# Routing of a two-layer mixture-of-experts block: the chain on PSUM, one comparison per one-hot matrix, the tokens' low parts behind it

## Chip, cores and metric

One core of one Trainium2 chip. The metric is the device time of one execution in microseconds (us), the median over several runs; lower is better. The five engines are named as the profile names them: PE (matrix), DVE (vector), ACT (scalar), POOL (GpSimd) and SP (whose queue issues nearly all DMAs); SPq is SP's queue, PEld the load of a matmul's stationary operand.

## What is computed

Two layers over 256 tokens x and 256 context tokens, width 1024. Each layer mixes tokens (gating, bidirectional retention) and then sends every token to 2 of 32 experts. The first layer routes 512 tokens, the second only the 256 of x. Cut to the routing:

```python
g_top, g_sel = lax.top_k(hf @ w_group + b_group, 1)            # 4 groups
e_in_group = take_along_axis(e_logits, g_sel)                  # 8 experts of that group
e_top, e_sel = lax.top_k(e_in_group, 2)
weights = p_group * softmax(e_top)
expert_id = g_sel * 8 + e_sel
y = sum over the 2 choices of weight * (silu(h @ w1[e]) * (h @ w3[e])) @ w2[e]
```

## The kernel before, in words

Tokens stand in tiles of 128: `nt` is 4 in layer 0 and 2 in layer 1. `split` (nt == 4) says that the tokens `h2[t]` are cut into a high part `h2h[t]` (ACT, `first_part`) and a low part `h2l[t]` (`second_part`, one subtraction of 128x1024), and that dispatch multiplies both with the one-hot matrices; in layer 1 `h2[t]` is used whole.

**Before the routing.** The last quarter of the output projection is made token tile by token tile. An order written out as a string sets what PE does: `o0` to `o3` are the four tiles (24 matmuls each, `out_tile`), `t` turns a finished tile for the router (`turned`, two transposes and an ACT copy) and finishes its norm (`final`, with a power on POOL, L186), `l` multiplies it with the router's weights into the PSUM bank `lob` (`logits`, L955), `r` and `R` do the same for the third quarter. After each tile DVE runs `residual` (L933, L935, L937).

**The routing chain on DVE**, L1046 to L1078: logits are summed and scaled in the SBUF tile `lr`, biases are added into `lo`; the best group by MAX8 and FIND_INDEX8 (`gm`, `gi`), its index as a float (`gf`, L1061), a mask over the groups (`goh`, L1063 and L1065), the masked logits (L1067), the two best experts (`em`, `ei`, `ef`), their one-hot rows `oh`, and the sum `ohs` in bf16. All of these tiles lie in SBUF. PE then counts with a triangular matrix how many earlier tokens chose each expert (`pp`, L1084) and the totals (`pc_`, L1088). At the same time POOL adds the shift to the last tile (`scaled`, L1003) and makes the low parts of tiles 0 to 2 (L1011, 128x1024 each); the low part of tile 3 is made on DVE behind the one-hot matrices.

**Places.** An expert has CAP = 64 places. DVE picks each choice's place out of `pp` (L1107, L1109), turns it into a slot number (`slot`, L1114, L1115), and `place` (L1119, L1120) builds the one-hot matrix `pm` of 128 slots with two comparisons per token tile against `iota`. In layer 0 four experts (a quad, 256 slots) are dispatched together (`quad_places`, `quad_block`, L1184), in layer 1 two (`pair_places`, `dispatch_some`, L1129). ACT copies the dispatched tokens into `xg`; then `expert` runs (`w1`, `w3`: L1220; `w2`: L1237), `weighted` scales (L1246, L1247), `collect` returns the result to the tokens (L1255, L1261, and additions on POOL, L1262).

**Order of work.** PE and SP run in program order. From the start of the routing to `routing.close()` DVE, ACT and POOL do too; after it a scheduler orders them. SP issues the experts' weights (0.5 MB each, 12 an expert) in one queue into a ring of buffers (`pump`); each waits until its buffer is free, and the next wait behind it. Some of these buffers held `h2[t]` before.

Of the kernel before, what the change touches and what calls it, by code (L numbers as in the profile page):

```python
# [21 lines left out]
P = 128  # L22
# [29 lines left out]
def hybrid_kernel(  # L52
# [481 lines left out]
    for l in range(depth):  # L534
# [451 lines left out]
        def out_tile(t):  # L986
            o = bank()
            for k in range(KD):
                ah, al = (a[:, t % 2 * P:(t % 2 + 1) * P] for a in mT[t // 2][k])
# [57 lines left out]
        V.tensor_tensor(out=lrv, in0=lrv, in1=rs4[:, 0:nt, None].to_broadcast([P, nt, 36]), op=ALU.mult)  # L1047
        V.tensor_tensor(out=lo[:, 0:nt, 0:36].rearrange("p (s t) e -> p s t e", t=2), in0=lrv.rearrange("p (s t) e -> p s t e", t=2),
# [12 lines left out]
        V.tensor_copy(gf[:, 0:nt], gi[:, 0:nt, 0:1])  # L1061
        goh = small([P, 4, GROUPS], tag="goh", bufs=1)
        V.tensor_tensor(out=goh[:, 0:nt], in0=iota[:, None, 0:GROUPS].to_broadcast([P, nt, GROUPS]),  # L1063
                        in1=gf[:, 0:nt].to_broadcast([P, nt, GROUPS]), op=ALU.is_equal)
        V.tensor_scalar(out=goh[:, 0:nt], in0=goh[:, 0:nt], scalar1=-LOW, scalar2=LOW, op0=ALU.mult, op1=ALU.add)  # L1065
# [3 lines left out]
                        in1=goh[:, 0:nt, :, None].to_broadcast([P, nt, GROUPS, PER_GROUP]), op=ALU.add)  # L1069
# [4 lines left out]
        V.tensor_copy(ef[:, 0:nt], ei[:, 0:nt, 0:2])  # L1074
        V.tensor_tensor(out=oh[:, 0:nt].rearrange("p t j e -> p (t j) e"),
                        in0=iota[:, None, 0:EXPERTS].to_broadcast([P, 2 * nt, EXPERTS]),
                        in1=ef[:, 0:nt].rearrange("p t j -> p (t j)")[:, :, None].to_broadcast([P, 2 * nt, EXPERTS]), op=ALU.is_equal)
        V.tensor_tensor(out=ohs[:, 0:nt], in0=oh[:, 0:nt, 0], in1=oh[:, 0:nt, 1], op=ALU.add)  # L1078
# [10 lines left out]

        negm = small([P, 4, 1], tag="negm", bufs=1)  # L1090
# [14 lines left out]
        pos = small([P, 8], tag="pos", bufs=1)
        for j in range(2):
            V.tensor_tensor(out=sel[:, 0:nt, j], in0=oh[:, 0:nt, j], in1=pp[:, 0:nt * EXPERTS].rearrange("p (t e) -> p t e", e=EXPERTS),  # L1107
                            op=ALU.mult)
        V.tensor_reduce(out=pos[:, 0:W], in_=selv, axis=X, op=ALU.add)  # L1109
        isov = small([P, 8], tag="isov", bufs=1)  # L1110
        V.tensor_scalar(out=isov[:, 0:W], in0=pos[:, 0:W], scalar1=float(CAP), scalar2=None, op0=ALU.is_ge)

        slot = small([P, 8], tag="slot", bufs=1)
        V.scalar_tensor_tensor(out=slot[:, 0:W], in0=efv, scalar=float(CAP), in1=pos[:, 0:W], op0=ALU.mult, op1=ALU.add)  # L1114
        V.scalar_tensor_tensor(out=slot[:, 0:W], in0=isov[:, 0:W], scalar=65536.0, in1=slot[:, 0:W], op0=ALU.mult, op1=ALU.add)  # L1115

# [49 lines left out]
        def quad_places(q):  # L1166
            pm = a4t((P, 4, 256), F32R)
            for i in range(2):
                base = small([P, 8], tag="base")
                V.tensor_scalar(out=base[:, 0:W], in0=slot[:, 0:W], scalar1=-128.0 * (2 * q + i), scalar2=None, op0=ALU.add)  # L1170
                place(base, P, pm[:, :, i * P:(i + 1) * P])
# [397 lines left out]
```

## Time and profile before

| | |
|---|---|
| median of 3 runs | 1930.32 us (1927.92 to 1930.35) |
| the profiled execution's own time | 1926.31 us |
| its span | 1924.5 us |
| busy in the span | PE 94%, DVE 50%, ACT 33%, POOL 27% |
| granted TensorE clock, mean | 0.977 |
| routing of layer 0, of layer 1 | about 563 to 594 us, about 1425 to 1443 us |

The span is what the trace covers; the device time of the same execution is 1.8 us longer. A timeline row gives start, duration, engine, line, operation, output<-input, count, and in brackets how long the engine stood idle before it and what ended that.

### The profile page before, as it was taken

The numbers are of one execution on the slowest core, as the hardware profiler recorded it, in microseconds if no ns is written. First come the engines' busy times: TensorE is split into PE (matmuls) and PEld (weight loads), VectorE is DVE, ScalarE is ACT, GpSimd is POOL, SyncE is SP. The second block draws the span as 40 slices with busy tenths as digits, with TensorE's granted clock in tenths as the row PEclk, the third lists the DMA queues.
The fourth block names the chain that finished last, engine by engine and source line by source line (L and its number), as shares of the span: only waits on it lengthen the run. The fifth ranks groups of instructions, "written<-read, shape, count | busy, mean of one in ns | idle before, by whom it ended". The sixth has DMA issues, their size and how long they took to land. (4 is left out here: it accounts for less than half of the span.)

```text
span 1924.5 us, 28311 instructions
## 1 busy us (share of the span) xinstructions
PE 1810.2 (94%) x10899; PEld 1238.4 (64%) x10899; DVE 958.7 (50%) x1748; ACT 629.6 (33%) x1012; POOL 524.3 (27%) x417
## 2 busy tenths in 40 slices
PE   7999998899977999999999889999979999999996
PEld 5988898798974444444444389999964444444442
DVE  4878575564554334333433377885562232232223
ACT  3645454443332121222122254444432221222222
POOL 1444353432030233232424242132021122122121
PEclk9999999899998999999999899999989999999998
DMA  9445343344765999999999549863798999999995
GB/s 342 133 165 181 121 154 126 115 154 148 207 227 179 396 405 402 402 402 403 406 402 391 188 162 321 281 197 122 233 346 306 406 409 409 409 409 408 409 409 220
DMA packets 234111, 553.49 MB, mean 288 GB/s; under 512 B 23121, under 2 KB 118513, under 8 KB 233970
## 3 DMA queue, kind: packets, MB, share of 16 engines
q1 hardware_dynamic: 233586, 551.57, 77.1%
q8 instruction: 88, 1.44, 0.3%
q14 instruction: 53, 0.43, 0.1%
q0 software_dynamic: 384, 0.05, 0.0%
HBM read 550.45 MB, written 1.10 MB: 287 GB/s over the span
## 5 line engine op out<-in xcount | busy, mean ns | idle before, releaser
L1262 POOL TENSOR_TENSOR u<-u,t 128x512 f32<-128x512 f32 x184 | 229.4, 1281 | 749.3 <-DVE t L1261 749.0
L1220 PE MATMUL mm<-u,a 128*64 128x512 f32 x1376 | 333.6, 593 | 1.4 <-ACT a L1132 1.4
L207 DVE TENSOR_TENSOR wlo<-raw,whi 128x1024 fp32r<-128x1024 f32 x157 | 218.2, 1392 | 152.1 <-ACT whi L206 151.7
L247 PE MATMUL mm<-u,wlo 128*128 128x256 f32 (+1 forms) x800 | 268.7, 336 | 5.4 <-DVE wlo L207 5.4
L245 PE MATMUL mm<-u,whi 128*128 128x256 f32 (+1 forms) x800 | 269.9, 337 | 0.0
L246 PE MATMUL mm<-u,whi 128*128 128x256 f32 (+1 forms) x800 | 267.6, 334 | 0.0
L1247 DVE SCALAR_TENSOR_TENSOR a<-mm,sw,a 64x512 fp32r<-64x512 f32 x128 | 95.9, 749 | 335.8 <-ACT a L1246 335.5
L245 PE MATMUL mm<-whi,u 128*128 128x256 f32 x832 | 240.0, 288 | 1.9 <-ACT u L569 1.5
L247 PE MATMUL mm<-whi,u 128*128 128x256 f32 x832 | 237.9, 286 | 0.8 <-DVE u L571 0.4
L246 PE MATMUL mm<-wlo,u 128*128 128x256 f32 x832 | 237.1, 285 | 0.8 <-DVE wlo L207 0.8
L1220 PEld LDWEIGHTS mm<-u,a 128*64 128x64 f32 x1376 | 106.3, 137 | 195.8 <-issue 178.1
L206 ACT ACTIVATE whi<-raw 128x1024 fp32r<-128x1024 f32 x160 | 169.7, 1063 | 170.3 <-PE mm L246 62.5
L1261 DVE TENSOR_TENSOR t<-mm,u 128x512 f32<-128x512 f32 x190 | 119.6, 675 | 135.2 <-PE mm L1255 134.8
L247 PEld LDWEIGHTS mm<-u,wlo 128*128 128x128 f32 x800 | 151.9, 190 | 22.7 <-DVE wlo L207 7.5
L245 PEld LDWEIGHTS mm<-whi,u 128*128 128x128 f32 x832 | 161.0, 193 | 6.8 <-issue 3.3
L1246 ACT ACTIVATE a<-mm,sw 64x512 fp32r<-64x512 f32 x128 | 87.3, 682 | 235.4 <-PE mm L1237 187.3
L245 PEld LDWEIGHTS mm<-u,whi 128*128 128x128 f32 x800 | 152.0, 190 | 17.2 <-issue 1.6
L1237 PE MATMUL mm<-u,t 128*64 128x512 f32 x664 | 157.3, 610 | 5.9 <-ACT t L1231 5.9
L247 PEld LDWEIGHTS mm<-whi,u 128*128 128x128 f32 x832 | 160.8, 193 | 2.2 <-DVE u L571 1.0
L246 PEld LDWEIGHTS mm<-wlo,u 128*128 128x128 f32 x832 | 161.0, 194 | 1.3 <-DVE wlo L207 1.2
L246 PEld LDWEIGHTS mm<-u,whi 128*128 128x128 f32 x800 | 152.0, 190 | 14.4
L1223 ACT ACTIVATE t<-mm 64x512 f32<-64x512 f32 x64 | 38.0, 594 | 322.3 <-PE mm L1220 322.3
(309 smaller groups left out, 2625.3 us busy)
## 6 DMA issues: line engine op xcount, KB each, us to landing
u<-in_w_dram SPq DMA_DIRECT2D x510, 512.0 KB
raw<-in_w_in_dram SPq DMA_DIRECT2D x96, 512.0 KB
raw<-in_w_dram SPq DMA_DIRECT2D x75, 512.0 KB
whi<-in_w_dram SPq DMA_DIRECT2D x73, 512.0 KB
wlo<-in_w_dram SPq DMA_DIRECT2D x73, 512.0 KB
a<-in_w_ada_dram SPq DMA_DIRECT2D x57, 512.0 KB
u<-in_w_ada_dram SPq DMA_DIRECT2D x39, 512.0 KB
a<-in_w_dram SPq DMA_DIRECT2D x37, 512.0 KB
```

The costliest lines, as they stand in the source:

```text
L206: S.activation(hi, rv, AF.Copy)
L207: low_by[0].tensor_tensor(out=lo, in0=rv, in1=hi.bitcast(F32), op=ALU.subtract)
L245: T.matmul(out, lhsT=sh, rhs=mh, start=first, stop=False)
L246: T.matmul(out, lhsT=sh, rhs=ml, start=False, stop=False)
L247: return T.matmul(out, lhsT=sl, rhs=mh, start=False, stop=last)
L1220: T.matmul(o[h * 64:(h + 1) * 64, :], lhsT=x[:, s0:s0 + 64], rhs=w(k), start=(k == 0), stop=(k == KD - 1), tile_position=(0, 64 * h))
L1223: S.activation(hh[0:64], o[64:128, :], AF.Silu)
L1237: T.matmul(o[n % banks][n * 64:(n + 1) * 64, :], lhsT=hTt[:, s], rhs=wc(s)[:, n * 512:(n + 1) * 512], start=(s == 0), stop=(s == 3), tile_ ...
L1246: S.activation(dh, src, AF.Copy, scale=w)
L1247: V.scalar_tensor_tensor(out=dl, in0=src, scalar=w, in1=dh.bitcast(F32), op0=ALU.mult, op1=ALU.subtract)
L1261: V.tensor_tensor(out=y, in0=o, in1=g2[t // 2][:, hs], op=ALU.mult)
L1262: eng.tensor_tensor(out=res[t][:, hs], in0=res[t][:, hs], in1=y, op=ALU.add)
```

## The change

1. In layer 0 the order string becomes `o0 r o1 R t0 o2 l0 t1 s0 O3 l2 t3 s1 l3`: tile 3 (`O3`) takes the logits of tile 1 and the turning of tile 2 between its matmuls. `scaled_at_once` (DVE) serves tiles 0 and 1; tiles 2 and 3 go by `scaled` (ACT, then POOL).
2. The chain's intermediate values lie in the bank `lob`.
3. `pp` plus one, times `ohs`, gives each token's place per expert (`far`, in `lob`; `where`, a copy in SBUF for later). `slots` builds a one-hot matrix with one comparison of this with 1 to 64.
4. POOL makes the low part of tile 0 only; tiles 1 to 3 are made on DVE behind the first one-hot matrices, and PE takes all high parts before the low ones.
5. What only the overflow needs (`pos`, `isov` and on) moves to `blocks()`; `routing.close()` comes after it.

```diff
-        for op in ("o0 r o1 R t0 o2 l0 t1 o3 l1 t2 l2 t3 l3" if nt == 4 else "o0 r t0 o1 R l0 t1 l1").split():
+        for op in ("o0 r o1 R t0 o2 l0 t1 s0 O3 l2 t3 s1 l3" if nt == 4 else "o0 r t0 o1 R l0 t1 l1").split():
...
+            elif op[0] == "O":
+                gate_c = out_tile(t, {2: lambda: last_logits(1), 5: lambda: last_turned(2)})
...
-        scaled(nt - 1)
+        for t in range(nt - 2, nt):
+            scaled(t)
         pump(PRE[l][2])
         if split:
             for t in range(nt):
                 first_part(t)
-            for t in range(nt - 1):
-                second_part(t, G)
-        lrv = lr[:, 0:nt]
-        V.tensor_tensor(out=lrv, in0=lrv, in1=lob[:, 0:nt * 36].rearrange("p (t e) -> p t e", e=36), op=ALU.add)
...
+            second_part(0, G)
+
+        lrv, lobv = lr[:, 0:nt], lob[:, 0:nt * 36].rearrange("p (t e) -> p t e", e=36)
+        V.tensor_tensor(out=lobv, in0=lobv, in1=lrv, op=ALU.add)
...
-        gf = small([P, 4, 1], tag="gf", bufs=1)
+        gf = lob[:, 144:144 + nt].rearrange("p (t o) -> p t o", o=1)
...
-        goh = small([P, 4, GROUPS], tag="goh", bufs=1)
+        goh = lob[:, 160:160 + nt * GROUPS].rearrange("p (t g) -> p t g", g=GROUPS)
...
+        far = lob[:, 0:nt * EXPERTS].rearrange("p (t e) -> p t e", e=EXPERTS)
+        V.scalar_tensor_tensor(out=far, in0=pp[:, 0:nt * EXPERTS].rearrange("p (t e) -> p t e", e=EXPERTS), scalar=1.0, in1=ohs[:, 0:nt],
+                               op0=ALU.add, op1=ALU.mult)
+        where = lr[:, :, 0:EXPERTS]
+
+        def slots(e0, n, pm, src, ts):
+
+            V.tensor_tensor(out=pm[:, ts, 0:n * CAP].rearrange("p t (e s) -> p t e s", e=n),
+                            in0=iota[:, None, None, 1:CAP + 1].to_broadcast([P, ts.stop - ts.start, n, CAP]),
+                            in1=src[:, ts, e0:e0 + n, None].to_broadcast([P, ts.stop - ts.start, n, CAP]), op=ALU.is_equal)
+
+        if split:
+            pm = a4t((P, 4, 256), F32R)
+            slots(0, 4, pm, far, slice(0, 2))
+            slots(0, 4, pm, far, slice(2, 4))
+            for t in range(1, nt):
+                second_part(t, V)
+        else:
+            pm = t2t((P, 4, P), F32R)
+            slots(0, 2, pm, far, slice(0, nt))
...
+            held0 = [bank() for _ in range(2)]
+            for part in range(2):
+                for k in range(4):
+                    for t in range(nt):
+                        T.matmul(held0[k // 2][:, k % 2 * 256:(k % 2 + 1) * 256],
...
-                routing.close()
...
                     blocks()
                     if last:
                         row_everywhere(g2[0])
+                    routing.close()
```

The instructions at three places. First DVE in layer 0, from the logits to the masked logits; `mm_5122` is the bank `lob`, `rs` the four norm factors, `rc` the biases. Before:

```order
L1046 TENSOR_TENSOR lr_4655<-lr_4655,mm_5122 128x144
L1047 TENSOR_TENSOR lr_4655<-lr_4655,rs_761_5121 128x144
L1048 TENSOR_TENSOR lo_601<-lr_4655,rc 128x4x36
L1057 MAX gm_5343<-lo_601 128x8 x4
L1059 MAX_INDEX gi_5344<-gm_5343,lo_601 128x8 x4
L1061 CAST gf_5355<-gi_5344 128x4
L1063 TENSOR_TENSOR goh_5357<-iota,gf_5355 128x16
L1065 TENSOR_SCALAR goh_5357<-goh_5357 128x16
L1067 TENSOR_TENSOR lr_4655<-lo_601,goh_5357 128x4x32
```

and now:

```order
L1056 TENSOR_TENSOR mm_5122<-mm_5122,lr_4655 128x144
L1057 TENSOR_TENSOR mm_5122<-mm_5122,rs_761_5121 128x144
L1058 TENSOR_TENSOR lo_601<-mm_5122,rc 128x4x36
L1067 MAX gm_5340<-lo_601 128x8 x4
L1069 MAX_INDEX gi_5341<-gm_5340,lo_601 128x8 x4
L1071 CAST mm_5122<-gi_5341 128x4
L1073 TENSOR_TENSOR mm_5122<-iota,mm_5122 128x16
L1075 TENSOR_SCALAR mm_5122<-mm_5122 128x16
L1077 TENSOR_TENSOR lr_4655<-lo_601,mm_5122 128x4x32
```

The same nine steps in the same order; seven of them now read or write the bank, and none of these seven reads two tiles of SBUF.

Second, DVE in layer 0 behind the counts of PE (`mm_5368` is `pp`, `a_800` the first `pm`, `u_801` to `u_803` the low parts of tiles 1 to 3), as it is now:

```order
L1104 SCALAR_TENSOR_TENSOR mm_5122<-mm_5368,ohs_4657 128x128
L1110 TENSOR_TENSOR a_800_5385<-iota,mm_5122 128x512 x2
L1013 TENSOR_TENSOR u_801_5388<-u_698_4651,u_790_5329 128x1024
L1013 TENSOR_TENSOR u_802_5390<-u_699_4652,u_791_5331 128x1024
L1013 TENSOR_TENSOR u_803_5392<-u_700_4653,u_792_5333 128x1024
L1125 COPY lr_4655<-mm_5122 128x4x32
L1127 TENSOR_SCALAR negm_5395<-gm_5340 128x4
L1131 TENSOR_TENSOR dex_5399<-em_5342 128x4
```

Three instructions stand where some thirty stood (with the sixteen comparisons L1119 and L1120 among them); behind them come three low parts instead of one, and `negm`, on which the exponentials of ACT (L1097, now L1133) wait, has moved from before the counts to behind the low parts.

Third, PE in layer 0 at the first dispatch. `u_789` to `u_792` are the high parts, `u_793` and on the low ones. Before (the first eight of 32):

```order
L1184 MATMUL mm_5434<-a_812_5409,u_789_5326 128x256
L1184 MATMUL mm_5434<-a_812_5409,u_793_5334 128x256
L1184 MATMUL mm_5434<-a_812_5409,u_790_5328 128x256
L1184 MATMUL mm_5434<-a_812_5409,u_794_5336 128x256
L1184 MATMUL mm_5434<-a_812_5409,u_791_5330 128x256
L1184 MATMUL mm_5434<-a_812_5409,u_795_5338 128x256
L1184 MATMUL mm_5434<-a_812_5409,u_792_5332 128x256
L1184 MATMUL mm_5434<-a_812_5409,u_817_5432 128x256
```

and now the last four of the sixteen high ones and the first four low ones:

```order
L1295 MATMUL mm_5411<-a_800_5385,u_789_5327 128x256
L1295 MATMUL mm_5411<-a_800_5385,u_790_5329 128x256
L1295 MATMUL mm_5411<-a_800_5385,u_791_5331 128x256
L1295 MATMUL mm_5411<-a_800_5385,u_792_5333 128x256
L1295 MATMUL mm_5410<-a_800_5385,u_793_5335 128x256
L1295 MATMUL mm_5410<-a_800_5385,u_801_5388 128x256
L1295 MATMUL mm_5410<-a_800_5385,u_802_5390 128x256
L1295 MATMUL mm_5410<-a_800_5385,u_803_5392 128x256
```

The eighth matmul needed the last low part; now the twentieth does.

## Rows read from the trace of the kernel before

**Rows 1.** Timeline, PE, layer 0: start us, us, work [idle before, releaser].

```profile
565.45 0.64 PE L955 MATMUL mm<-wr,t 128*128 128x36 f32 x4 [1.23 <-ACT t L949]
...
580.53 0.21 PE L1084 MATMUL mm<-ohs,upper 128*128 128x32 bf16 x1 [13.09 <-DVE ohs L1078]
...
586.06 2.31 PE L1184 MATMUL mm<-a,u 128*128 128x256 f32 x7 [4.98 <-DVE a L1120]
588.86 4.78 PE L1184 MATMUL mm<-a,u 128*128 128x256 f32 x25 [0.49 <-DVE u L1011]
593.57 1.94 PE L1220 MATMUL mm<-u,a 128*64 128x512 f32 x8
...
607.71 0.43 PE L1229 MATMUL mm<-ident,t 64*128 64x64 f32 x4 [1.58 <-DVE t L1224]
```

**Rows 2.** Timeline, DVE, layer 0.

```profile
563.64 0.43 DVE L933 TENSOR_TENSOR mm<-mm,t 128x256 f32<-128x256 f32 x1 [0.67 <-PE mm L247]
...
568.82 2.35 DVE L1048 TENSOR_TENSOR lo<-lr,rc 128x144 f32<-128x144 f32 x1
...
572.16 1.25 DVE L1061 CAST gf<-gi 128x4 f32<-128x4 uint32 x1
573.44 2.27 DVE L1063 TENSOR_TENSOR goh<-iota,gf 128x16 f32<-128x16 f32 x1
575.74 2.26 DVE L1065 TENSOR_SCALAR goh<-goh 128x16 f32<-128x16 f32 x1
578.04 0.29 DVE L1067 TENSOR_TENSOR lr<-lo,goh 128x128 f32<-128x128 f32 x1
...
580.18 0.29 DVE L1078 TENSOR_TENSOR ohs<-oh 128x128 bf16<-128x128 f32 x1
...
587.59 1.22 DVE L1011 TENSOR_TENSOR u<-u,u 128x1024 fp32r<-128x1024 f32 x1
...
606.17 0.69 DVE L1209 TENSOR_REDUCE sw<-mm 64x1 f32<-64x2 f32 x4 [4.14 <-PE mm L1205]
```

**Rows 3.** Timeline, POOL, layer 0, the routing.

```profile
568.62 2.39 POOL L1003 TENSOR_TENSOR u<-u,u 128x1024 f32<-128x1024 f32 x1 [1.26 <-ACT u L1002]
570.97 7.00 POOL L1011 TENSOR_TENSOR u<-u,u 128x1024 fp32r<-128x1024 f32 x3
```

**Rows 4.** Timeline, DVE, layer 0, in the experts.

```profile
670.12 4.25 DVE L1261 TENSOR_TENSOR t<-mm,u 128x512 f32<-128x512 f32 x7
```

**Rows 5.** Timeline, POOL, layer 0, in the experts.

```profile
669.68 9.93 POOL L1262 TENSOR_TENSOR u<-u,t 128x512 f32<-128x512 f32 x8 [22.96 <-DVE t L1261]
```

**Rows 6.** Timeline, ACT, layer 0: the first and the last of the exponentials.

```profile
580.59 0.30 ACT L1097 ACTIVATE ge<-lo,negm 128x4 f32<-128x4 f32 x1 [6.96 <-DVE negm L1091]
...
582.15 0.19 ACT L1098 ACTIVATE dex<-dex 128x4 f32<-128x4 f32 x1
```

**Rows 7.** Timeline, DVE, layer 1, the routing.

```profile
1429.20 2.26 DVE L1048 TENSOR_TENSOR lo<-lr,rc 128x72 f32<-128x72 f32 x1
...
1432.11 1.58 DVE L1061 CAST gf<-gi 128x2 f32<-128x2 uint32 x1
```

**Rows 8.** Timeline, PE, layer 1, the routing.

```profile
1435.89 0.19 PE L1084 MATMUL mm<-ohs,upper 128*128 128x32 bf16 x1 [7.32 <-DVE ohs L1078]
...
1438.38 3.91 PE L1129 MATMUL mm<-t,u 128*128 128x128 f32 x16 [2.20 <-DVE t L1120]
```

**Rows 9.** Timeline, POOL, layer 1, the routing.

```profile
1428.99 4.67 POOL L1003 TENSOR_TENSOR u<-u,u 128x1024 f32<-128x1024 f32 x2 [0.87 <-ACT u L1002]
```

**Rows 10.** Stretches: busy us of each engine, granted clock, DMA share, GB/s.

```profile
591.00:593.00 2.00, 2.00 (x13) 2.00 (x13) 0.00 (x0) 0.60 (x1) 0.00 (x0) 0.67 0.33 133
...
1750.00:1800.00 50.00, 49.32 (x256) 21.90 (x254) 14.04 (x33) 10.94 (x19) 5.28 (x5) 1.00 1.03 408
```

**Rows 11.** Waits of SP's queue, 560:1060: us in total, times, longest.

```profile
SPq L274 <- PE mm L1237: 168.9, 112, 5.6
```

**Rows 12.** The same in layer 1, 1400:1924.

```profile
SPq L274 <- DMA u<-in_w_dram: 188.3, 210, 1.9
```

More of the change, by code (lines that the diff above doesn't have):

```diff
@@ L984, in hybrid_kernel, with out_tile @@
         pump(PRE[l][1])
-        def out_tile(t):
+        def out_tile(t, amid=None):
             o = bank()
             for k in range(KD):
+                if amid and k in amid:
+                    amid[k]()
                 ah, al = (a[:, t % 2 * P:(t % 2 + 1) * P] for a in mT[t // 2][k])
@@ L1073, in hybrid_kernel @@
             V.max_index(ei[:, t], em[:, t], ein[:, t])
[L1074 to L1078, printed above, removed]
+        W = 2 * nt
+        efp = lob[:, 192:192 + W].rearrange("p (t j) -> p t j", j=2)
+        V.tensor_copy(efp, ei[:, 0:nt, 0:2])
+        ohp = lob[:, 320:320 + nt * EXPERTS].rearrange("p (t e) -> p t e", e=EXPERTS)
+        for j, dst in ((1, ohp), (0, oh[:, 0:nt, 0])):
+            V.tensor_tensor(out=dst, in0=iota[:, None, 0:EXPERTS].to_broadcast([P, nt, EXPERTS]),
+                            in1=efp[:, :, j:j + 1].to_broadcast([P, nt, EXPERTS]), op=ALU.is_equal)
+        V.tensor_tensor(out=ohs[:, 0:nt], in0=ohp, in1=oh[:, 0:nt, 0], op=ALU.add)
         pp = bank()
@@ L1088, in hybrid_kernel @@
             T.matmul(pc_[:, 0:EXPERTS], lhsT=ones_bf, rhs=ohs[:, t], start=(t == 0), stop=(t == nt - 1))
+        far = lob[:, 0:nt * EXPERTS].rearrange("p (t e) -> p t e", e=EXPERTS)
[15 more added lines that the diff above has]
+            slots(0, 2, pm, far, slice(0, nt))
+        V.tensor_copy(where[:, 0:nt], far)
         negm = small([P, 4, 1], tag="negm", bufs=1)
@@ L1098, in hybrid_kernel @@
         S.activation(dex[:, 0:nt], dex[:, 0:nt], AF.Exp)
-        W = 2 * nt
-        sel = t2t((P, 4, 2, EXPERTS))
-        selv = sel[:, 0:nt].rearrange("p t j e -> p (t j) e")
+        V.tensor_copy(oh[:, 0:nt, 1], ohp)
+        V.tensor_copy(ef[:, 0:nt], efp)
         ohv = oh[:, 0:nt].rearrange("p t j e -> p (t j) e")
         efv = ef.rearrange("p t j -> p (t j)")[:, 0:W]
[L1105 to L1115, printed above, removed]
         def place(base, n, dst):
@@ L1167, in quad_places @@
             pm = a4t((P, 4, 256), F32R)
[L1168 to L1171, printed above, removed]
+            slots(4 * q, 4, pm, where, slice(0, nt))
             return pm
@@ L1190, in pair_places @@
         def pair_places(pr):
-            base = small([P, 8], tag="base")
-            V.tensor_scalar(out=base[:, 0:W], in0=slot[:, 0:W], scalar1=-128.0 * pr, scalar2=None, op0=ALU.add)
-            return places(base, P)
+            pm = t2t((P, 4, P), F32R)
+            slots(2 * pr, 2, pm, where, slice(0, nt))
+            return pm
         def combine_parts(pm, n, w, pt=None):
@@ L1269, in hybrid_kernel @@
         if split:
-            pm = quad_places(0)
             xg = [quad_tiles(), None]
-            second_part(3, V)
-            held0 = []
-            for k in range(4):
-                quad_block(pm, xg[0], k, held0)
+            held0 = [bank() for _ in range(2)]
[3 more added lines that the diff above has]
+                        T.matmul(held0[k // 2][:, k % 2 * 256:(k % 2 + 1) * 256],
+                                 lhsT=(h2l if part else h2h)[t].rearrange("t (a p j) -> t a j p", p=P, j=2)[:, k // 2, k % 2], rhs=pm[:, t],
+                                 start=(k % 2 == 0 and t == 0 and part == 0), stop=(k % 2 == 1 and t == nt - 1 and part == 1))
+            for k in range(0, 4, 2):
+                S.activation(xg[0][0][:, k:k + 2], held0[k // 2].rearrange("p (k n) -> p k n", k=2), AF.Copy)
         else:
-            pm = pair_places(0)
             xg = [a4t((P, KD, P)), None]
@@ L1317, in blocks @@
             ost = small([P, 8], tag="ostart", bufs=1)
+            sel = t2t((P, 4, 2, EXPERTS))
+            selv = sel[:, 0:nt].rearrange("p t j e -> p (t j) e")
+            pos = small([P, 8], tag="pos", bufs=1)
+            isov = small([P, 8], tag="isov", bufs=1)
+            for j in range(2):
+                V.tensor_tensor(out=sel[:, 0:nt, j], in0=oh[:, 0:nt, j], in1=where[:, 0:nt], op=ALU.mult)
+            V.tensor_reduce(out=pos[:, 0:W], in_=selv, axis=X, op=ALU.add)
+            V.tensor_scalar(out=pos[:, 0:W], in0=pos[:, 0:W], scalar1=-1.0, scalar2=None, op0=ALU.add)
+            V.tensor_scalar(out=isov[:, 0:W], in0=pos[:, 0:W], scalar1=float(CAP), scalar2=None, op0=ALU.is_ge)
             V.tensor_tensor(out=selv, in0=ohv, in1=os2[:, None, :].to_broadcast([P, W, EXPERTS]), op=ALU.mult)
```

36 lines of the change are left out of this document (18 added, 18 removed).

## Prediction

> **What bounds the kernel now.** I read the busy shares first (PE 94%), then PE's timeline, to see where PE stands still, and at each pause the engine it waits for. Around layer 0's routing PE has its longest pauses: 13.09 us until DVE has `ohs`, 4.98 until the first one-hot matrix is there, 0.49 for the last low part; the first expert's matmuls begin at 593.57 [rows 1]. In layer 1 the same pauses are 7.32 and 2.20 [rows 8]. So DVE's chain is the path there. Why it is long stands in DVE's own timeline: four tiny steps take 2.35, 1.25, 2.27 and 2.26 us, while L1067, larger than three of them, takes 0.29 [rows 2]. The reader should lay POOL's rows beside them: POOL works from 568.62 to 577.97 in four operations of 2.3 to 2.4 us [rows 3], and each of the four steps ends within 0.2 us behind the end of one of these (their starts and mean length give 571.0, 573.3, 575.6 and 578.0). They wait for POOL; nothing they need comes from it. In layer 1 L1048 and L1061 (2.26 and 1.58) end behind POOL's two operations in the same way [rows 7, 9]. Last I asked whether time won here reaches the end. In layer 0's experts SP's queue waits above all for PE to free buffers [rows 11], so the stream of weights follows PE. In layer 1 it waits for its own transfers [rows 12], and the DMA engines are full (408 GB/s) beside a full PE [rows 10]: there it is a question, taken up below.
>
> All times are made against the profiled execution (1926.31 us, span 1924.5), which lies 4.0 below the median of 1930.32; the sum is then taken from the median. A measurement of this kernel can tell about 0.2%, 4 us, from no change.
>
> **Layer 0, step by step.**
>
> *Tile 3.* Six small matmuls move into it. Behind it the same matmuls waited 1.23 us for an ACT copy [rows 1]; inside it PE would wait for such a copy too, with 24 matmuls queued behind. I put tile 3 1.3 us later: 0.5 for the matmuls and most of such a wait (bounds 0.5 and 1.8). In return one of two scalings of 128x1024 between tile 3 and the logits leaves DVE, about 1.2 by the operation of that size (L1011) [rows 2]. From L933 to L1048 lie now 5.2 us [rows 2]; so L1058 starts at 563.64 + 1.3 + 5.2 - 1.2 = 568.9, as L1048 does. Nothing won.
>
> *The chain.* POOL is as busy as before in this stretch: two shifts and one low part, three operations instead of four. The four steps sum to 8.13 us. If an operand in PSUM frees them, each costs at most what L1067 does, 0.29: 1.16 in all, 7.0 less. One comparison more costs 0.3. `ohs` is there at 580.47 - 6.7 = 573.8. No row shows a step that writes into PSUM from SBUF beside a busy POOL. The bounds are 0 (still held, rival A) and 8; the nearest row is L1261, which reads PSUM and one SBUF tile: seven in 4.25 us, 0.61 each, inside a stretch in which POOL works without a break [rows 4, 5]. I take the freed value.
>
> *One-hot matrices.* From the counts to the first dispatch lie now 586.06 - 580.53 = 5.5 us [rows 1]. The new path: PE's counts 0.5 (matmuls of 0.2 that overlap), L1104 0.3 (the size of L1067), two comparisons of 128x512 at L1261's 0.61. Together 2.0: the first half is there at 575.2, all at 575.8.
>
> *Low parts.* DVE makes three, 3 x 1.22 = 3.7, until 579.5; the last one used to be there at 587.59 + 1.22 = 588.8. PE takes the sixteen high ones meanwhile, at the 4.78 / 25 = 0.19 us that the same matmuls took [rows 1]: 575.2 + 0.6 of waiting + 3.0 = 578.8. From 579.5 thirteen low ones are left, 2.5: PE is done at 582.0.
>
> *The copy to `xg`.* A new wait: ACT's exponentials stand ahead of the copy and now wait for `negm`, which stands behind the low parts. `negm` is there at 579.5 + 0.5; the exponentials take 582.34 - 580.59 = 1.75 [rows 6]; the copy 0.6 (ACT's busy time in [rows 10], where it makes one such copy). 582.35 for the first expert matmul, against 593.57: **11.2 us won**. Without this queue on ACT, PE's own end would allow a bit earlier.
>
> *In expert 0.* PE waited 1.58 for L1224, which stood on DVE behind four reductions (0.69) and their wait for PE [rows 1, 2]. L1244 now stands ahead of them, since the hand-written order reaches that far. Between 0.69 and 1.58; I take **1.0**.
>
> **Layer 1.** L1048 and L1061 go from 3.84 to at most 0.58, less 0.2 for one comparison more: `ohs` 3.1 earlier, 1432.8. Then counts 0.3, L1104 0.3, one comparison of 128x256 at 0.4 (two thirds of L1261's): 1433.8 instead of 1438.38. POOL's shift, which the matmuls need too, ends at 1428.99 + 4.67 = 1433.7 [rows 9], so no more is to be had. **4.6 won.**
>
> **Costed at nothing.** What goes to `blocks()`, some 14 DVE steps, lies beside PE's dense work, where DVE is busy 14 of 50 us [rows 10]; without that cover 14 x 0.29 = 4 us a layer. Later quads: one comparison of 128x1024 (1.2) for sixteen, earlier done than before; POOL can hold it up by one of its additions, 9.93 / 8 = 1.24 [rows 5], which costs only where PE is already waiting for it. On SP, the buffer of tile 0 heads the queue and comes free with POOL's third operation instead of its second, 2.3 later; it takes one of expert 1's last weights, not due for some 15 us. Tiles 1 to 3 come free by 579.5 instead of 588.8.
>
> **The sum:** 11.2 + 1.0 + 4.6 = 16.8. Profiled execution 1909.5; median 1930.3 - 16.8 = **1913.5 us**.
>
> [...] The rows show DVE held up by POOL, never what a DVE step with two SBUF inputs does to POOL. [...]
>
> **Rivals.**
> A. *PSUM does not free DVE*, so the change doesn't do what it says. Then L1058, L1071 and L1073 still wait for POOL's three operations: 2.35 + 1.25 + 2.27 - 3 x 0.29 = 5.0 of layer 0's gain is lost, and 3.3 of layer 1's. 16.8 - 8.3 = 8.5: 1921.8. For it: every held step ends with a POOL operation, and none of them had PSUM. Against it: L1261 [rows 4].
> [...]
> C. *The weights take layer 1's gain.* For it: the full DMA engines and [rows 12]. Against: SP's queue is blocked behind PE while the ring is full, and that wait shrinks with PE's. If nothing passes: 1918.1.
> D. *The stream is the bound in both layers*; then PE waits later for what it gained: 1930. Against: [rows 11].
> [...]
>
> **How the numbers follow.** Forecast 0.71, A 0.09, B 0.06, C 0.07, D 0.03, E 0.04. Faster by over 0.2%: the forecast, A, B and C, 0.93; within: D, 0.03; slower: E, 0.04. The range goes down to 1906: 0.8 if tile 3 loses only 0.5, 0.6 if all of the 1.58 goes, some 0.8 if the freed steps cost less than 0.29, 1.0 if ACT's queue costs less, and 4.0 because one execution lay that far below the median. Up to 1922 it takes in A, B and C.
>
> **What would show it.** Right: the steps L1058, L1071, L1073 and L1075 at 0.3 or less beside busy POOL rows; PE's pause before the counts near 6 us in layer 0 and 4 in layer 1; the first expert matmuls some 11 us sooner behind tile 3's start; the exponentials right ahead of the copy to `xg`; the last weights landing earlier by the whole sum. Wrong: any of those steps at 1 us or more; POOL's L1013 behind DVE's; PE waiting for weights in layer 1; a clock under 0.9 in expert 0; pauses of PE for quad matrices.

## Result, and the profile after

The changed kernel takes 1906.04 us (four runs, 1905.24 to 1907.06) against 1930.34: a ratio of 0.9872, 95% interval 0.9856 to 0.9888, or 24.3 us less. Measured a second time it gave 0.9859 (0.9842 to 0.9877). The forecast was 16.8 us less, 1913.5, with a range from 1906 to 1922: the direction was right, the size too small by 7.5, and the ratio times the time before, 1905.6, lies just outside the range.

The profiled execution took 1907.06 us, its span is 1905.3, its mean granted clock 0.981. What answers to [rows 1], PE's timeline in layer 0 of the changed kernel (L1097 are the counts, L1295 the first dispatch, L1240 `w1` and `w3`, L1249 the transposes, L1257 `w2`):

```profile
575.82 0.21 PE L1097 MATMUL mm<-ohs,upper 128*128 128x32 bf16 x1 [5.50 <-DVE ohs L1091]
...
577.47 5.94 PE L1295 MATMUL mm<-a,u 128*128 128x256 f32 x32 [1.10 <-DVE a L1110]
583.92 1.94 PE L1240 MATMUL mm<-u,a 128*64 128x512 f32 x8 [0.51 <-ACT a L1299]
...
596.99 0.46 PE L1249 MATMUL mm<-ident,t 64*128 64x64 f32 x4 [0.51 <-DVE t L1244]
...
598.30 3.65 PE L1257 MATMUL mm<-a,t 128*64 128x512 f32 x16
```

The pauses of 13.09, 4.98 and 0.49 have become 5.50 and 1.10, the one of 1.58 in expert 0 has become 0.51. DVE there, to lay beside [rows 2]:

```profile
571.22 0.31 DVE L1058 TENSOR_TENSOR lo<-mm,rc 128x144 f32<-128x144 f32 x1
...
572.51 0.17 DVE L1071 CAST mm<-gi 128x4 f32<-128x4 uint32 x1
572.71 0.18 DVE L1073 TENSOR_TENSOR mm<-iota,mm 128x16 f32<-128x16 f32 x1
572.92 0.18 DVE L1075 TENSOR_SCALAR mm<-mm 128x16 f32<-128x16 f32 x1
...
576.64 1.28 DVE L1110 TENSOR_TENSOR a<-iota,mm 128x512 fp32r<-128x512 f32 x2
577.84 3.49 DVE L1013 TENSOR_TENSOR u<-u,u 128x1024 fp32r<-128x1024 f32 x3
```

and POOL, to lay beside [rows 3]:

```profile
570.81 4.66 POOL L1005 TENSOR_TENSOR u<-u,u 128x1024 f32<-128x1024 f32 x2
575.43 2.35 POOL L1013 TENSOR_TENSOR u<-u,u 128x1024 fp32r<-128x1024 f32 x1
```

POOL works from 570.81 to 577.8 without a break, and the four steps that took 2.35, 1.25, 2.27 and 2.26 beside it now take 0.31, 0.17, 0.18 and 0.18. The low parts on DVE end at 581.33. On ACT the exponentials stand right ahead of the copy to `xg`, as forecast:

```profile
581.64 0.30 ACT L1133 ACTIVATE ge<-lo,negm 128x4 f32<-128x4 f32 x1 [3.78 <-DVE negm L1127]
...
583.30 1.06 ACT L1299 ACTIVATE a<-mm 128x512 f32<-128x512 f32 x2
```

In layer 1, beside [rows 8], the pauses of 7.32 and 2.20 are 4.08 and 0.82:

```profile
1420.40 0.18 PE L1097 MATMUL mm<-ohs,upper 128*128 128x32 bf16 x1 [4.08 <-DVE ohs L1091]
...
1421.51 3.51 PE L1152 MATMUL mm<-t,u 128*128 128x128 f32 x16 [0.82 <-DVE lr L1125]
```

SP's queue waits much as before. In 560:1060 the wait for `w2` of [rows 11] stands at 170.8; in 1400:1924 the wait of [rows 12] stands at 190.0. For the low parts, which free the buffers of `h2[t]`, the queue waited four times in the kernel before:

```profile
SPq L274 <- POOL u L1011: 11.9, 3, 8.1
SPq L274 <- DVE u L1011: 10.5, 1, 10.5
```

and now it waits once for POOL, and 2.4 us in all for DVE:

```profile
SPq L274 <- PE mm L1257: 170.8, 115, 5.7
...
SPq L274 <- POOL u L1013: 9.3, 1, 9.3
```

The last `w2` begins at 1886.05 instead of 1904.20, so the stream passed the gain on.

**Where the time went.** The pauses on the path account for about 17 us. For the rest I took the stretches in which the granted clock is low: in the profile of the kernel before it is 0.50 in each half us from 590 to 592 and 1.00 in those from 592.5 to 593.5. Here are PE's rows in expert 0 and two stretches of 2 us from a profile of the kernel before (before_look1 below; columns as in [rows 10]):

```profile
608.68 0.43 PE L1229 MATMUL mm<-ident,t 64*128 64x64 f32 x4 [1.59 <-DVE t L1224]
...
609.97 5.35 PE L1237 MATMUL mm<-a,t 128*64 128x512 f32 x16
```

```profile
610.00:612.00 2.00, 2.00 (x7) 0.55 (x8) 0.63 (x4) 0.33 (x1) 0.00 (x0) 0.64 1.01 344
612.00:614.00 2.00, 2.00 (x8) 0.73 (x6) 0.00 (x0) 0.00 (x0) 0.00 (x0) 0.51 0.44 170
```

PE is busy all the time, but at a mean granted clock of 0.64 in the first stretch and 0.51 in the second. Busy time times what the clock lacks of full is 2.00 x 0.36 + 2.00 x 0.49 = 1.70 us, and that is what the sixteen matmuls took too long: 5.35 against the 3.65 of the changed kernel. Added up over all stretches of 2 us with a clock under 0.97, I call this a profile's **lost time**. For five profiles of the kernel before and four of the changed one:

| profile | time | span | lost | span less lost |
|---|---|---|---|---|
| before | 1926.3 | 1924.5 | 23.1 | 1901.4 |
| before_again | 1928.1 | 1926.3 | 25.7 | 1900.6 |
| before_look1 | 1933.4 | 1931.5 | 31.6 | 1899.9 |
| before_look2 | 1929.0 | 1927.2 | 26.1 | 1901.1 |
| before_look3 | 1933.0 | 1931.2 | 29.6 | 1901.6 |
| after | 1907.1 | 1905.3 | 22.3 | 1883.0 |
| after_again | 1906.9 | 1905.1 | 20.6 | 1884.5 |
| after_look1 | 1907.7 | 1905.8 | 22.1 | 1883.7 |
| after_look2 | 1906.2 | 1904.4 | 19.9 | 1884.5 |

The last column is steady within 2 us for each kernel: 1900.9 and 1883.9 in the mean, **17.0 us of path**. The lost time is 27.2 and 21.2 in the mean, **6.0 us of clock**. Executions of one kernel differ by their lost time and hardly by anything else. Together that is 23.0 us, the difference of the mean spans of these profiles; the medians differ by 24.3, and by 26 by the mean of the two ratios. The 1 to 3 us beyond 23.0 no profile shows.

### The profile page after: what moved, and what is told of

It reads as the page before. It is cut to its first block, busy times and chain, and to the rows that moved or that the text cites. A ratio compares the mean times of both kernels' runs of the same rounds, so it can differ in the third digit from the quotient of the medians.

```text
span 1905.3 us, 28120 instructions
## 1 busy us (share of the span) xinstructions
PE 1808.8 (95%) x10899; PEld 1239.2 (65%) x10899; DVE 911.3 (48%) x1558; ACT 630.9 (33%) x1013; POOL 529.5 (28%) x416
## 5 line engine op out<-in xcount | busy, mean ns | idle before, releaser
L1282 POOL TENSOR_TENSOR u<-u,t 128x512 f32<-128x512 f32 x184 | 236.0, 1319 | 722.8 <-DVE t L1281 722.8
L1240 PE MATMUL mm<-u,a 128*64 128x512 f32 x1376 | 333.6, 592 | 1.9 <-ACT a L1155 1.4
L1240 PEld LDWEIGHTS mm<-u,a 128*64 128x64 f32 x1376 | 106.2, 137 | 196.3 <-issue 177.6
L1257 PE MATMUL mm<-u,t 128*64 128x512 f32 x664 | 155.5, 604 | 5.9 <-ACT t L1251 5.9
```

The costliest lines, as they stand in the source:

```text
L1240: T.matmul(o[h * 64:(h + 1) * 64, :], lhsT=x[:, s0:s0 + 64], rhs=w(k), start=(k == 0), stop=(k == KD - 1), tile_position=(0, 64 * h))
L1257: T.matmul(o[n % banks][n * 64:(n + 1) * 64, :], lhsT=hTt[:, s], rhs=wc(s)[:, n * 512:(n + 1) * 512], start=(s == 0), stop=(s == 3), tile_ ...
L1282: eng.tensor_tensor(out=res[t][:, hs], in0=res[t][:, hs], in1=y, op=ALU.add)
```

## Experiments

Differences are taken from the ratios to the kernel before, which was measured anew beside the runs; the change stands at 0.9866 in the mean of its two. 0.001 is 1.9 us.

**1. The kernel before, again** (no edit).

> The kernel before, once more, for a second profile. The change gained 24.3 us by the medians, but the two profiled executions differ by 19.2 only (1926.3 and 1907.1). Theory 1: the remaining 5 are executions of the kernel before that lose time somewhere outside the change's two stretches; its times then lie at 1926 to 1933 again, and a profile above 1928 shows one place with a longer wait. Theory 2: the profiled execution was the odd one; then the times lie at 1930 to 1933 and the second profile shows every stage a little longer. Both: the granted clock drops again to its lower level in expert 0 behind the pause of 1.58 us at the transposes of L1229.

1930.37 us, 1928.12 to 1934.0 in ten runs, ratio 0.9998 (0.9988 to 1.0007). The second profile has the drop in expert 0 again, 1.72 us lost at 610 to 616. Both theories were too coarse: it is neither one wait nor every stage. Three further profiles settled it:

> The kernel before, one more profiled execution. Both profiles so far are of executions below the median (1926.3 and 1928.1 against 1930 to 1934). Counted as PE's busy time at less than full clock they lost 23.1 and 25.7 us; without that both would span 1901 (1901.4 and 1900.6). Theory: an ordinary execution of the kernel before differs from these by the clock alone: its span less its lost time is again 1901 within 1, and an execution of 1932 shows some 29 lost, in more stretches behind PE's pauses. Rival: it is another wait (transfers, the start), and the span less the lost time then lies above 1903.

Span less lost time is 1899.9, 1901.1 and 1901.6 at times of 1933.4, 1929.0 and 1933.0. The executions differ by the clock; what is left agrees within 1.7. The mean granted clock says the same without a profile: in the runs of the kernel before it goes from 0.976 at 1928 to 0.972 at 1935.

**2. The changed kernel, again** (no edit).

> The changed kernel once more, unaltered, for its spread. By the stretches of lower granted clock in the profiles so far, the changed kernel's execution lost 22.3 us to the lower clock (PE's busy time times what is missing from full clock, in steps of 2 us), those of the kernel before 23.1 and 25.7. With these taken off, the spans differ by 1900.9 - 1883.0 = 18 us, and the medians by 24. Theory 1: the change also takes some 6 us of lower clock away in an ordinary execution; then the times stay at 1905 to 1908 with a mean granted clock of 0.980 to 0.982, against 1928 to 1936 at 0.972 to 0.976 before. Theory 2: the four executions seen were lucky; then more of them lie at 1908 to 1913 with a clock of 0.977 to 0.979, and the gain shrinks to about 20.

1905.96 (1904.28 to 1909.96), clock 0.979 to 0.983. Theory 1 held. Two more profiles were to show whether the loss is steady:

> One more profile of the changed kernel. Five profiles of the kernel before span 1899.9 to 1901.6 once their time at lower clock (23.1 to 31.6) is taken off; two of the changed one span 1883.0 and 1884.5 and lost 22.3 and 20.6. Theory: 1884 within 1 again, with 20 to 23 lost, of which 2.3 to 2.4 at layer 0's routing and expert 0 (4.9 to 5.2 before). Rival: the loss varies as before's does, and this execution loses 25 or more.

22.1 and 19.9 us are lost, 2.2 of it at layer 0's routing and expert 0 both times. The loss is steady.

**3. The chain back in SBUF.**

```diff
-        gf = lob[:, 144:144 + nt].rearrange("p (t o) -> p t o", o=1)
+        gf = small([P, 4, 1], tag="gf", bufs=1)
...
-        goh = lob[:, 160:160 + nt * GROUPS].rearrange("p (t g) -> p t g", g=GROUPS)
+        goh = small([P, 4, GROUPS], tag="goh", bufs=1)
...
```

(and the sum of the logits, `ef` and `oh` likewise).

> The changed kernel with the chain's intermediate values back in SBUF, all else kept. Theory: the bank in PSUM alone freed DVE from POOL. Then the logits with biases, the index as a float and the mask are held again by POOL's three operations, as rival A has it: 2.35 + 1.25 + 2.27 - 3 x 0.29 = 5.0 us in layer 0 and 3.3 in layer 1, so 1906.0 + 8.3 = 1914.3; PE's pause before the counts goes from 5.50 to 10.5 and from 4.08 to 7.3. Rival: it was POOL's shorter work (one low part in place of three) that freed DVE; then the pauses stay at 5.5 and 4.1 and the time at 1906.

1918.41, ratio 0.9930 (0.9915 to 0.9945). PE waits 10.55 and 7.32 us before the counts:

```profile
580.52 0.21 PE L1095 MATMUL mm<-ohs,upper 128*128 128x32 bf16 x1 [10.55 <-DVE ohs L1088]
...
1429.09 0.19 PE L1095 MATMUL mm<-ohs,upper 128*128 128x32 bf16 x1 [7.32 <-DVE ohs L1088]
```

On DVE the steps are held again:

```profile
570.53 2.45 DVE L1057 TENSOR_TENSOR lr<-lr,rs 128x144 f32<-128x144 f32 x1 [0.21 <-POOL rs L186]
573.01 2.34 DVE L1058 TENSOR_TENSOR lo<-lr,rc 128x144 f32<-128x144 f32 x1
...
576.34 1.25 DVE L1071 CAST gf<-gi 128x4 f32<-128x4 uint32 x1
```

They end at 572.98, 575.35 and 577.59, within 0.2 us of where POOL's operations of that run end (its L1005 x2 from 570.46 takes 4.72, its L1013 from 575.15 takes 2.41). The theory holds in the size of both pauses; POOL's shorter work alone frees none of them. Span less lost time is 1892.2, 8.3 more than the changed kernel's mean and just the forecast. The time rises by 12, so some 4 of it is not path.

**4. The chain in PSUM alone, in the kernel before** (the edit of 3, the other way round; copies of `oh` and `ef` into SBUF behind `ohs`).

> The kernel before with the chain in PSUM and nothing else of the change. Theory of the separate parts: 7.0 us in layer 0 and 3.1 in layer 1 are won, 1930.3 - 10.1 = 1920.2. Rival: the parts need each other. POOL's low parts still run until 577.97, and the places behind the counts, some thirty small steps on SBUF, now begin at 574 instead of 581, beside POOL; if those are held as the chain was, they get going at 578, and of layer 0's 7.0 only 581.0 - 578.0 = 3 us remain: 1930.3 - 3 - 3 = 1924. The rows of L1109 to L1120 tell which, and which forms of step are held.

1925.08, ratio 0.9965 (0.9953 to 0.9976), 6.8 less: short of the theory's 10.1 and near the rival's 6, and the rival's mechanism is there. `ohs` comes 7 us earlier, and then DVE is held at the next steps that read and write SBUF, while POOL makes its three low parts:

```profile
574.57 2.04 DVE L1096 TENSOR_SCALAR negm<-gm 128x4 f32<-128x4 f32 x1
...
576.60 0.47 DVE L1111 TENSOR_TENSOR t<-oh,mm 128x128 f32<-128x128 f32 x2
577.11 0.42 DVE L1113 TENSOR_REDUCE pos<-t 128x8 f32<-128x256 f32 x1
577.56 1.36 DVE L1115 TENSOR_SCALAR isov<-pos 128x8 f32<-128x8 f32 x1
```

```profile
571.93 6.96 POOL L1011 TENSOR_TENSOR u<-u,u 128x1024 fp32r<-128x1024 f32 x3
```

By their mean length POOL's three end at 574.25, 576.57 and 578.89; `negm` ends at 576.61 and `isov` at 578.92. What is not held is as telling: the product that reads a bank (0.47 for its two), and the reduction (0.42), though it reads and writes SBUF. Held beside POOL are, in these two runs, the tensor_scalar between SBUF tiles here (`negm` 2.04 and `isov` 1.36, against 0.16 and 0.17 in the kernel before, behind POOL's work), and in run 3 the two steps that read two SBUF tiles (2.45 and 2.34, against 0.32 and 0.31 with the bank in the changed kernel) and the cast (1.25 against 0.17).

So the parts of the change need each other: the later places are won only because `negm`, `isov` and the rest no longer stand ahead of them beside POOL.

**5. The places as before, in the changed kernel** (`slot`, `place` and `quad_places` of the kernel before, chain and low parts as changed).

> The changed kernel with the places made as before: slot numbers out of the counts, sixteen comparisons for the first one-hot matrix of layer 0 and four of layer 1, two a token tile for all later ones; chain in PSUM, tile 3 and low parts stay as changed. Theory: from the counts to the first dispatch in layer 0 PE waits 5 instead of 1.1 us; the three low parts on DVE stand behind the sixteen comparisons, 583.4 + 3.5 instead of 577.8 + 3.5, so the first expert matmul is 5 to 6 us later, and in layer 1 1.4 later: 1906 + 7 = 1913. Beside POOL some of the small steps are held as well (POOL's last operation ends at 577.8), which can add up to 2. Rival: the rows behind the counts are not the limit since POOL's low part and ACT's copies end at the same time; then 1906 + 3.

1916.95, ratio 0.9909 (0.9892 to 0.9926), 8.3 more than the change, where 7 was forecast. PE waits 5.31 for the one-hot matrices:

```profile
581.81 7.67 PE L1304 MATMUL mm<-a,u 128*128 128x256 f32 x32 [5.31 <-DVE a L1125]
589.41 1.94 PE L1249 MATMUL mm<-u,a 128*64 128x512 f32 x8
```

From tile 0's logits (L955) to the first expert matmul it is 27.06 instead of 21.69, 5.4 more, and layer 1's dispatch comes 1.4 later. The theory holds.

**6. The low parts as before, in the changed kernel.**

```diff
-            second_part(0, G)
+            for t in range(nt - 1):
+                second_part(t, G)
...
-            for t in range(1, nt):
-                second_part(t, V)
+            second_part(3, V)
```

(and `quad_block` for the first four blocks).

> The changed kernel with the low parts as before: tiles 0 to 2 on POOL, tile 3 on DVE, high and low matmuls of a tile taken in turn. Theory: POOL's last low part is there at 577.8 + 2 x 2.35 = 582.5 instead of DVE's at 581.3, and PE, which needs it for its sixth matmul, stands still from about 578 to 582.5 with 27 matmuls left (5.1 at the lower clock): expert 0 starts at 588 instead of 583.9, 4 us later: 1910, and up to 2 more by the clock. Rival: the order of high and low is worth little, since POOL's five operations and PE's matmuls overlap; 1907.

1915.77, ratio 0.9920 (0.9899 to 0.9942), 10 more, where the theory had 4 and up to 2 by the clock. PE's rows show the two waits, and expert 0 starts 5.1 later:

```profile
580.15 0.80 PE L1204 MATMUL mm<-a,u 128*128 128x256 f32 x2 [1.52 <-POOL u L1013]
583.43 5.66 PE L1204 MATMUL mm<-a,u 128*128 128x256 f32 x27 [2.48 <-POOL u L1013]
```

Span less lost time is 1887.0, only 3.1 above the changed kernel's mean, with 28.4 lost: so the path's share was near the forecast, and the clock's, some 7, was far above it. This run also shows that DVE and POOL hold each other up in both directions, in DVE's one low part beside POOL's three:

```profile
577.85 3.33 DVE L1013 TENSOR_TENSOR u<-u,u 128x1024 fp32r<-128x1024 f32 x1
```

```profile
575.44 7.94 POOL L1013 TENSOR_TENSOR u<-u,u 128x1024 fp32r<-128x1024 f32 x3
```

DVE's takes 3.33 instead of 1.22, and POOL's three take 0.94 more than the 7.00 of [rows 3]. The changed kernel escapes this because POOL starts its only low part 2.4 us before DVE's first, and it takes 2.35.

**7. Tile 3 as before, in the changed kernel** (order string `... s0 o3 l1 t2 s1 l2 t3 s2 l3`).

> The changed kernel with the old order of tile 3 (its 24 matmuls apart, logits of tile 1 and the turning of tile 2 behind it, the scaling of tile 2 on DVE again), all else kept. The step of the prediction: tile 3 pays 1.3 and wins 1.2 back on DVE, so nothing is won by it. Counted from the last logits the counts came 6.6 us later with the old order and the chain in PSUM, and come 6.0 later in the changed kernel, whose last logits stand 1.5 later. Theory 1: 1.5 - 0.6 = 0.9 us earlier at the counts and at the first expert matmul, so 1905. Theory 2 (what the prediction says): no difference at the counts, 1906. Rival: the two transposes and logits back behind tile 3 make one more pause of 1.2 us, behind which the granted clock falls once more, and the time is 1908.

1906.62 (1905.72 to 1911.44), ratio 0.9883 (0.9863 to 0.9902): not told from the change. From tile 0's logits to the counts 13.48 against 13.58, to the first expert matmul 21.59 against 21.69. The forecast's "nothing won" for this part is right to 0.1 us, span less lost time is 1884.1, and my theory 1 was wrong.

**8. The hand-written order ending early, in the changed kernel** (`routing.close()` back in `rest_of_quad` and `rest_of_pair`).

> The changed kernel with the hand-written order ending where it did before, so that the scheduler again puts the four reductions ahead of the product L1244 in expert 0. Both theories: PE's pause before the transposes goes from 0.51 back to about 1.6 us, 1.07 lost. Theory 1, the clock: that pause is also what let the granted clock fall to its lower level in expert 0 of the kernel before (L1237 x16 took 5.35 us there and 3.65 now); then 1.7 more is lost, 1906.0 + 2.8 = 1908.8, and the sixteen matmuls of w2 take some 5.3 us. Theory 2: the clock fell for another reason (the earlier routing pauses); then 1907.1 and the sixteen matmuls stay at 3.65.

1917.18 (1911.09 to 1918.52; two of the six runs at 1911), ratio 0.9913 (0.9898 to 0.9928), 9 more, where both theories had 1 to 3. The profiled execution took 1918.5. PE in expert 0:

```profile
595.41 0.59 PE L1249 MATMUL mm<-ident,t 64*128 64x64 f32 x4 [1.58 <-DVE t L1244]
...
597.62 5.97 PE L1257 MATMUL mm<-a,t 128*64 128x512 f32 x16
```

The pause is 1.07 longer, as both say, and the clock falls behind it, to 0.50 in 596:602 of this profile, where 597:602 of the changed kernel's stands at 1.00: from the transposes (L1249) to the end of `w2`, with the matmuls of L1219 and L1225 between them, it takes 3.2 us longer. In layer 1 the same order costs another 0.9 (the transposes of experts 0 and 1 come 0.6 and 0.9 later behind the last logits, lost time taken off). The rest is lost time at other pauses: 31.4 is lost in this profile, and span less lost time is 1885.4. And the reverse, in the kernel before:

> The kernel before with the hand-written order of DVE, ACT and POOL reaching to the overflow's preparation in expert 1, as in the changed kernel, and nothing else. Theory: expert 0's pause of 1.58 goes to 0.5 (1.1 us), layer 1's transposes come 0.9 earlier, and the drop of the granted clock in expert 0's w2 (5.35 against 3.65) goes with the pause: 1.1 + 0.9 + 1.7 = 3.7 less than the kernel before. Rival: the order is worth 2.0 and the clock falls all the same.

1927.65 (1923.02 to 1931.68, twelve runs), ratio 0.9983 (0.9972 to 0.9994): 3.3 less, from 1 to 5. The pause is 0.5 and expert 0 has no drop:

```profile
609.29 0.46 PE L1229 MATMUL mm<-ident,t 64*128 64x64 f32 x4 [0.51 <-DVE t L1224]
...
610.61 3.65 PE L1237 MATMUL mm<-a,t 128*64 128x512 f32 x16
```

The transposes of layer 1's experts come earlier by 0.6 and 0.9. So in this profile the drop goes with the pause, as forecast, but the interval can't exclude the rival's 2.0, and the shorter path is not shown: this profile's span less lost time is 1902.8, not below the 1899.9 to 1901.6 of the kernel before. From the first expert matmul of layer 0 to the last logits of layer 1 it is 2.6 us longer than before's mean, lost time taken off. Part of that has a place: in expert 1 the next quad's dispatch now takes 2.93 instead of 2.19, as it does in run 5: with the old comparisons PE waits there for its one-hot matrix, another place where the parts need each other. The rest I did not trace.

A pause is not enough to say that the clock will fall: in run 4 the same pause of 1.59 before the transposes was followed by `w2` at 3.65.

**9. PE kept at work in its pauses, in the kernel before.**

```diff
+        def warm(o, n):
+            for _ in range(n):
+                T.matmul(o[:, 128:256], lhsT=ident, rhs=iota, start=True, stop=True)
...
         pp = bank()
+        warm(pp, 54 if split else 30)
```

(also 20 and 8 behind the totals, 6 before expert 0's transposes).

> The kernel before with PE kept at work in its pauses around the routing: matmuls of the identity with a constant into unused columns of PSUM, 54 and 20 of them in layer 0's two long pauses, 6 in expert 0's pause of 1.58, 30 and 8 in layer 1's. No step on the path changes. Theory (each long pause costs twice, itself and the lower clock behind it): the granted clock stays at 1.00 from 568 to 614 and in 1428 to 1444; the 25 dispatch matmuls take 2.9 instead of 4.78 to 5.0, w2 of expert 0 takes 3.65 instead of 5.35, layer 1 gains 0.5 to 2: 1931 - 5 = 1926. Rival (the drops of the clock follow from something else than PE's pauses): the drops stay, and the time is 1931 or, where the added matmuls run over a pause, more.

1924.4 (1923.02 to 1928.3), ratio 0.9956 (0.9942 to 0.9971), 8.5 less, with the same steps on the path. Span less lost time is 1901.1, that of the kernel before, and 21.5 is lost instead of 27.2. The added matmuls fill the pause (x108, since each is recorded as two), the dispatch starts where it did, and `w2` of expert 0 runs at full clock:

```profile
568.47 12.30 PE L1083 MATMUL mm<-iota,ident 128*128 128x128 f32 x108
...
590.07 4.77 PE L1190 MATMUL mm<-a,u 128*128 128x256 f32 x25 [0.68 <-DVE u L1011]
...
610.14 3.65 PE L1245 MATMUL mm<-a,t 128*64 128x512 f32 x16
```

The 25 dispatch matmuls still took 4.77, with the clock at 0.83 in 590:600: there the theory was wrong, the clock fell once more behind PE's waits of 0.43 and 0.68. In layer 1 the first expert matmul comes 1.4 earlier behind the logits. So the pauses that were filled cost the kernel before 6 to 11 us by the clock alone, beside their own length; 1.7 of it shows in expert 0 and 1.4 in layer 1, and the rest has no place that I could name.

**10. Versions that might beat the change.** First the exponentials ahead of the places (`negm`, `dex` and the exponentials before L1104) with added matmuls:

> The changed kernel with two edits: negm and the exponentials ahead of the places, so that ACT is free when the first half of the dispatched tokens is ready, and PE kept at work in the pauses that are left (22 and 4 added matmuls in layer 0, 16 and 2 in layer 1). Theory: the first copy to xg starts at the end of bank 0's matmuls instead of 583.30, the granted clock is 1.00 in 576 to 584, and PE comes to expert 0 about 1.0 to 1.3 us earlier; layer 1 gains up to 1.6 by the clock: 1906 - 2.5 = 1903.5. Rival: DVE's low parts, which end at 581.33, and not PE's clock or ACT set the start of expert 0; then 0.3 or less in layer 0 and 1905.

1906.71, ratio 0.9860 (0.9843 to 0.9877): not told from the change. The rows speak against the theory: from tile 0's logits to the first expert matmul it is 22.42 instead of 21.69, 0.7 later and not 1.0 to 1.3 earlier. The added matmuls ran over the pause (44 records took 6.79 us, 0.15 each where those of run 9 took 0.11, which I put down to the clock, and the counts come 7.09 instead of 6.14 behind the last logits), and `negm`, moved beside POOL, is held:

```profile
573.02 2.15 DVE L1110 TENSOR_SCALAR negm<-gm 128x4 f32<-128x4 f32 x1
```

It ends at 575.17, with POOL's low part (572.79 + 2.35). Behind the low parts, where the change has it, `negm` takes 0.16. Fewer added matmuls with the same order (light_warm: 12 and 4, 8 and 2, and 5 before three late pauses of layer 0's experts) gave 1905.36 (1903.07 to 1909.23), not told from the change. Then tile 3's old order, `negm` where the change has it, and the light filling:

> The changed kernel with tile 3's old order (worth 0.9 us on the path by the profile of that run), the exponentials where the change put them, and added matmuls in PE's pauses: 12 and 4 in layer 0's routing, 8 and 2 in layer 1's, 5 each before the transposes of experts 29 and 31 and before w2 of expert 30 of layer 0. Theory: 0.9 by the order and 2 to 3 by the clock: 1906 - 3.5 = 1902.5, the fastest of all. Rival: the lower clock comes at other pauses instead; 1905.

1902.57 (1901.58 to 1903.87, four runs), ratio 0.9850 (0.9829 to 0.9871): each of its runs is faster than each of the ten of the changed kernel (1904.28 to 1909.96), though the intervals of the ratios overlap. Some of the difference stands in layer 1, where the sixteen dispatch matmuls take 2.12 us instead of 3.51. But 1.4 to 2.7 us of the profile's lead is there before any edit acts: tile 0's logits stand at 560.13, against 561.48 to 562.85 in the changed kernel's profiles. And the 0.9 for the order is not borne out behind them, where run 7 shows 0.1. How much of this gain is the edit's is open.

## Why the prediction fell short

Point by point, in intervals from tile 0's logits (layer 0) or the last logits (layer 1), lost time taken off, means of five and four profiles:

- *Tile 3, nothing won:* right (run 7).
- *The chain, `ohs` 6.7 earlier:* right; the counts come 7.0 earlier, and the operands in PSUM are the cause (runs 3, 4). Rival A is out.
- *One-hot matrices, low parts, copy to `xg`, 11.2:* 11.0. The exponentials do delay the copy, PE waits 0.51 for it. B, in which POOL's low part comes behind DVE's three, did not occur: POOL's starts at 575.43, DVE's first at 577.84. What the two cost each other where they overlap is seen in run 6.
- *In expert 0, 1.0:* 1.08 at the pause. It can't be found further on: from the first expert matmul to layer 1's last logits the two kernels take 826.3 us each, lost time taken off.
- *Layer 1, 4.6:* 4.7 at the first expert matmul. 0.9 more comes in experts 0 and 1 from the later end of the hand-written order, which I had priced in layer 0 only, and 1.1 at the very end, where PE's last wait of 2.58 is 1.52. What is left over, some 1.8, is given back, ahead of layer 0's routing and between the layers; I can't name its cause.
- *What was costed at nothing* made no pause that I found, but with 1.0 missing between the layers it is not shown that all of it stayed hidden. Rivals C and D are out: the last `w2` begins 18.15 us earlier.

The sum of these is the 17.0 of the table, against 16.8. The parts up to the first expert matmuls were right by their mechanism; that the whole path came out so close is also luck, since the 2.0 that I had not priced and the 1.8 given back cancel.

**The step that failed is the sum's last one**, "the sum is then taken from the median", as if a pause cost its length alone. A term was missing: the time that PE's work takes longer at a lowered clock (0.50 at its lowest in run 8's profile) behind its pauses, 27.2 us before and 21.2 after. The stretch 591:593 in [rows 10] showed it (0.67), and I gave it no term in the sum, only the 0.04 for a slower kernel (E). No run of the record is slower than the kernel before, and the changed kernel's clock is 1.00 in expert 0 (597:602). I had the sign wrong: with fewer and shorter pauses, 6.0 us less is lost. By place, before and after: layer 0's routing and expert 0 4.9 to 5.2 and 2.2 to 2.4; layer 1's routing and first experts 2.2 to 6.0 and 1.6 to 4.2; the change of layers 4.5 to 9.3 and 3.2 to 5.9; the end 1.3 to 1.7 and 0 to 1.2. Of the first, 1.7 lies in expert 0 and is the change's own doing: run 8 brings the drop back with the pause in the changed kernel and takes it away with the pause in the kernel before, and run 9 takes it away by filling the pause. The rest of it, some 1 us in the routing, goes with the shorter pauses there, but no run sets it apart. The other places vary from one execution to the next, and why the changed kernel loses less there too is open. Undoing single parts of it raises both terms, the path and the loss:

| run | undone | span less lost | lost |
|---|---|---|---|
| mean of four | nothing | 1883.9 | 21.2 |
| 3 | chain in PSUM | 1892.2 | 23.2 |
| 5 | places | 1891.6 | 24.0 |
| 6 | low parts | 1887.0 | 28.4 |
| 8 | end of the order | 1885.4 | 31.4 |

The low loss of the changed kernel is easily disturbed, and not in proportion to the path.

The range failed with it: its lower end took the 4.0 us by which the profiled execution lay below the median as noise of the measurement, where it was lost time that a change of pauses can remove.

## What to carry to other kernels

Where PE is the bound, price a pause twice: its length, and the matmuls behind it, which may run at a lowered clock (here the sixteen of `w2` took 5.35 us behind a pause of 1.59, and 3.65 behind an equal one in run 4); taking the lost time off each profile before comparing makes executions agree within 2 us here that differ by 7. In this kernel the DVE steps that crawled beside a busy POOL were freed by operands in PSUM (four of them took 8.13 us, and now 0.84); but look at once for the next step of a held form behind it, since the wait moved there in run 4 (`negm`, 2.04). When one part of a change is tested alone, the parts may need each other: the PSUM chain alone brought 6.8 of 24 us.

## What the runs showed that I had not expected

- The time of one execution of the kernel before varies from 1926.3 to 1935.8. In the five that were profiled (1926.3 to 1933.4) the clock explains it: 23.1 to 31.6 us lost, the rest the same within 2.
- Drops of the clock come behind pauses of only 1.6 us and cost 1.7 us there (`w2` 5.35 against 3.65) or, with the matmuls ahead of `w2`, 3.2 (`w2` 5.97); behind an equal pause in run 4 none came.
- Useless matmuls in the pauses made the kernel before 8.5 us faster (0.9956), though no step of the path moved; where too many of them ran over the pause and `negm` was held besides (run 10), expert 0 started 0.7 later.
- Of DVE's steps beside POOL, a tensor_scalar of 128x4 took 2.04 to 2.15 us, a reduction of 128x256 0.42.
